# Norm before weights, and one more quad in seven products: a change to a decoder layer's order of work

## The chip, the core and the metric

The kernel runs on one NeuronCore of a Trainium2 chip. The core has five engines with queues of their own that meet only through semaphores: TensorE (PE, with its weight loads shown as PEld), VectorE (DVE), ScalarE (ACT), GpSimd (POOL) and SyncE (SP); in this kernel SP and POOL mainly issue DMAs. The metric is device time in microseconds of one execution. The profile is one execution, taken apart by a hardware profiler.

## The reference

One decoder layer on 256 tokens of width 2048, all in float32: a half-step SwiGLU feed-forward block, a mixer of two attention branches, and a second half-step feed-forward block, each followed by a residual sum and a layer norm.

```python
h = _layer_norm(ALPHA * h + 0.5 * _swiglu(h, ffn1_w_gate[l], ffn1_w_up[l], ffn1_w_down[l]), ln1_g[l], ln1_b[l])
mix = _mixer(h, ...)          # w_in, low-rank attention, differential attention, gates, w_out
h = _layer_norm(ALPHA * h + mix, ln2_g[l], ln2_b[l])
h = _layer_norm(ALPHA * h + 0.5 * _swiglu(h, ffn2_w_gate[l], ffn2_w_up[l], ffn2_w_down[l]), ln3_g[l], ln3_b[l])

def _swiglu(x, w_gate, w_up, w_down):
    return (jax.nn.silu(x @ w_gate) * (x @ w_up)) @ w_down
```

The hidden width of a feed-forward block (FFN) is 5632. Nearly all of the work is in products of the 256 tokens with large weight matrices, each of which is read once.

## The kernel before

**Precision and one product.** Every operand of a large product is split into a rounded part and a remainder, both in a faster 32-bit format: `split` (L151) lets ScalarE cast (L152, "CAST" in the profile) and VectorE subtract (L153). A product of two 128-blocks is then three matmuls, high by high, high by low, low by high: `triple`, L205, L206, L207. The split weights lie in `wring`, a ring of pairs of buffers; activations are called x, h, h1, y, xs in the profile (numbers are left out, so `h` there is a hidden quad of an FFN as well as the normed rows h1 and h2).

**Units.** The work is cut into units, one block of weights of 128x1024 each (two k-tiles of 128 by 512 columns). A unit has three steps: its load (on SP's queue), its preparation (the split, preceded by an add where blocks are combined) and its products. `unit`, `advance` and `look` (L170 to L195) let loads run three units and preparations four units ahead of the products. The two halves of the tokens are "blocks" b = 0 and b = 1 of 128 tokens. In `project` (L209) a unit's products for block 0 come at once, and those for block 1 are put into `behind` and follow up to LAG = 5 units later, so that block 0 of a layer's result is done well before block 1 and its norm can run beside the rest; `catch_up(n)` issues all but n of those left over. `later(n, fn)` runs fn after n more units have gone through. What is written in this order gets its final place on each engine from a planner, which simulates the engines and lets an instruction of lower rank go first if it would be ready sooner; `tc.issue_after(i)` forces that what is traced within stands behind instruction i on i's engine.

**Seven instead of eight.** Parts of the products use a scheme of Strassen's kind: a 2x2 product of blocks in seven block products instead of eight, with sums of the weights (VectorE, L405 in `Hybrid`, L595 in `Sliced`) and of the activations (`Seven`, `Extra`, `QuadForms`). `Hybrid` does the gate and up products and parts of the mixer. `Sliced` does an FFN's down product: 11 quads of the hidden width (a quad is 4 k-tiles of 128) in two passes p = 0 and p = 1 over half of the output columns each. In each pass quads 0 to 2 are in seven products ("s" in the string `mix`, 6 matmuls each) and the other eight in plain units ("p", 12 matmuls each); `order` gives the order of the seven products of a quad. A product's weight blocks "11", "12" and "22" lie in one buffer each (`self.R`), which products read and add to in place, and which is loaded again for the next quad once the last of them has read it. The rows of the hidden quads go through DRAM to be transposed and are fetched by `get_h` on POOL's queue; `split_h` splits them, `QuadForms.steps` makes the seven forms. In the last eight units of the second pass the blocks are apart as in `project`. `SLOTS` = 41 buffers are shared by all of the larger tiles.

**The norms.** `LayerNorm` holds the residual rows z, adds the results to them (`fold` L737, `evac` L749 and L751), counts (`bn_stats`, L754, L760) and, when a block's last part has come, runs `apply` (L764): mean and variance, `rstd` (L657: a square root on ScalarE, some small steps on VectorE), the normed rows (L784), then for each of the four quads of columns `rows_to_quad` (L644): four transposes on TensorE into a PSUM bank (L647; three banks), four scalings by gain and shift on ScalarE (L652), and the split into the next stage's x. `finish` (L788) makes the rows for the next residual sum (L790, L791). The norm's rows of gains and shifts are loaded on POOL's queue (L729) at the turns `at[1]`.

At the first FFN's end and after `w_out` the units of the next projection are written straight after the last ones, so the leftovers of block 1 alternate with the next projection's units, and block 1's norm is written five units later. `behind_x=3` holds back, in the second FFN's first projection alone, the splits of units 3 and later behind the split of the normed quad 0 of block 0 (`x.made[0, 0]`). In the mixer's groups over `Hybrid` with `small` set, the last results stand behind the last split (`behind_split`, L333).

## Time and profile before

| | us |
|---|---|
| median of three runs (1981.73 to 1983.7) | 1982.71 |
| the profiled execution's own time | 1981.89 |
| its span in the profile | 1979.8 |
| first norm: first transposes (L647) | 689.2 |
| second norm: second block's transposes (L647) | 1296.1 |
| second FFN's last unit's products end | 1969.1 |

The page gives for each engine its busy time, its share of the span and its number of instructions. A busy TensorE says that a matmul was under way, not that it ran at its peak; ends of matmuls are modelled, so lost time is better counted from the distance of their starts. Windows give the same numbers for a stretch of time, the waits say which instruction ended another engine's idle time, and the rows of the timeline merge neighbouring instructions of one kind (xN), with the idle time before them in brackets.

### The profile page before, as it was taken

To read this page: it belongs to the slowest core of one execution; us is meant where nothing else is said; L and a number is where in the kernel's file an instruction comes from. 1 tells how busy PE (TensorE), PEld (TensorE's weight loads), DVE (VectorE), ACT (ScalarE), POOL (GpSimd) and SP (SyncE) were. 2 spreads that over 40 slices of the span, in tenths; PEclk is the share of its full clock that TensorE was granted. 3 is DMA by queue.
4 is the path that set the end of the run, shared out by engine and by line. 5 is a ranking of instruction groups with operands and counts; after the bars stand their busy time and mean duration, and the time that the engine had idled before them with its cause. 6 is when DMAs were issued, how large, how long until landed. Compare 5 with 4: busy or idle time off the path is not lost.

```text
span 1979.8 us, 25620 instructions
## 1 busy us (share of the span) xinstructions
PE 1960.8 (99%) x8796; PEld 1621.2 (82%) x8796; DVE 1756.0 (89%) x2135; ACT 1261.4 (64%) x1637; POOL 294.3 (15%) x515
## 2 busy tenths in 40 slices
PE   9999999999999999999999999999999999999997
PEld 7888888888888798888788888878888888888886
DVE  7999999999998889998877676699999999989886
ACT  6666666766655566666667765566676666666552
POOL 0221112112100011002223120012112121121000
PEclk9999999999999999999999999999999999999999
DMA  8978888778777666677667667579888877787763
GB/s 303 292 234 272 273 257 252 226 221 316 252 231 260 216 214 242 220 250 250 219 209 249 232 216 273 183 245 289 240 290 268 243 241 238 214 323 256 245 214 125
DMA packets 144594, 484.63 MB, mean 245 GB/s; under 512 B 20640, under 2 KB 20688, under 8 KB 144464
## 3 DMA queue, kind: packets, MB, share of 16 engines
q1 hardware_dynamic: 112752, 389.60, 57.2%
q0 software_dynamic: 31712, 93.41, 17.7%
q8 instruction: 69, 1.13, 0.2%
q14 instruction: 61, 0.50, 0.1%
HBM read 454.08 MB, written 28.84 MB: 244 GB/s over the span
## 4 chain that ended last, share of the span: by engine, by line
PE 48%; DVE 3%; issue 1%; DMA 1%; ACT 1%; POOL 0%; DVEq 0%; POOLq 0%; ACTq 0%
PE mm L206 15%; PE mm L207 15%; PE mm L205 15%; DVE wring L153 2%; DVE sraw L405 1%; DMA turn<-blocks 1%; PE tr L205 0%; PE tr L207 0%; PE tr L206 0%; POOL turn L684 0%; ACT wring L152 0%; DMA turned<-turn 0%; DVE blocks L682 0%; PE tr L1229 0%; PE tr L1231 0%
## 5 line engine op out<-in xcount | busy, mean ns | idle before, releaser
L152 ACT CAST wring<-raw 128x1024 fp32r<-128x1024 f32 (+2 forms) x475 | 490.6, 1038 | 340.7 <-PE mm L207 249.4
L153 DVE TENSOR_TENSOR wring<-raw,wring 128x1024 fp32r<-128x1024 f32 (+2 forms) x475 | 566.9, 1200 | 121.1 <-ACT wring L152 118.1
L152 ACT CAST wring<-sraw 128x1024 fp32r<-128x1024 f32 x436 | 452.0, 1051 | 191.9 <-DVE sraw L405 76.5
L153 DVE TENSOR_TENSOR wring<-sraw,wring 128x1024 fp32r<-128x1024 f32 x436 | 520.9, 1218 | 26.7 <-ACT wring L152 24.6
L207 PE MATMUL mm<-wring,h 128*128 128x512 f32 (+2 forms) x1260 | 484.7, 385 | 0.0
L206 PE MATMUL mm<-wring,h 128*128 128x512 f32 (+2 forms) x1260 | 484.3, 385 | 0.1
L205 PE MATMUL mm<-wring,h 128*128 128x512 f32 (+2 forms) x1260 | 483.8, 385 | 0.4 <-ACT h L152 0.4
L206 PE MATMUL mm<-wring,xs 128*128 128x512 f32 x776 | 303.1, 391 | 1.8 <-DVE wring L153 1.2
L205 PE MATMUL mm<-wring,xs 128*128 128x512 f32 x776 | 302.3, 390 | 0.0
L207 PE MATMUL mm<-wring,xs 128*128 128x512 f32 x776 | 302.0, 389 | 0.0
L206 PEld LDWEIGHTS mm<-wring,h 128*128 128x128 f32 x1260 | 236.7, 188 | 47.7 <-DVE wring L153 1.4
L205 PEld LDWEIGHTS mm<-wring,h 128*128 128x128 f32 x1260 | 236.7, 188 | 47.4 <-ACT h L152 0.9
L207 PEld LDWEIGHTS mm<-wring,h 128*128 128x128 f32 x1260 | 236.7, 188 | 47.2 <-DVE h L153 0.7
L405 DVE TENSOR_TENSOR sraw<-sraw,sraw 128x1024 f32<-128x1024 f32 x168 | 199.3, 1217 | 3.5 <-DMA sraw<-in_wdv_dram 2.4
L206 PEld LDWEIGHTS mm<-wring,xs 128*128 128x128 f32 x776 | 145.7, 188 | 35.7 <-DVE wring L153 5.6
L205 PEld LDWEIGHTS mm<-wring,xs 128*128 128x128 f32 x776 | 145.7, 188 | 30.3
L207 PEld LDWEIGHTS mm<-wring,xs 128*128 128x128 f32 x776 | 145.7, 188 | 29.8
L206 PE MATMUL mm<-wring,x 128*128 128x512 f32 x348 | 135.9, 390 | 0.7 <-DVE wring L153 0.7
L205 PE MATMUL mm<-wring,x 128*128 128x512 f32 x348 | 135.1, 390 | 0.7 <-ACT wring L152 0.5
L207 PE MATMUL mm<-wring,x 128*128 128x512 f32 x348 | 135.3, 389 | 0.0
L684 POOL DMA_DIRECT2D hT<-blocks x176 | 96.8, 562 | 186.4 <-DVE blocks L682 186.4
L407 POOL DMA_DIRECT2D sraw<-in_gu_dram x40 | 35.5, 887 | 511.7 <-DVE sraw L405 406.2
(301 smaller groups left out, 2210.4 us busy)
## 6 DMA issues: line engine op xcount, KB each, us to landing
raw<-in_gu_dram SPq DMA_DIRECT2D x167, 512.0 KB, 5.1
sraw<-in_gu_dram SPq DMA_DIRECT2D x160, 512.0 KB, 5.3
raw<-in_dn_dram SPq DMA_DIRECT2D x140, 512.0 KB, 4.8
sraw<-in_gu_dram POOLq DMA_DIRECT2D x40, 512.0 KB, 7.0
sraw<-in_dn_dram SPq DMA_DIRECT2D x36, 512.0 KB, 6.2
hraw<-hT POOLq DMA_DIRECT2D x68, 256.0 KB, 5.7
raw<-in_w_out_dram SPq DMA_DIRECT2D x32, 512.0 KB, 4.3
eraw<-in_gu_dram SPq DMA_DIRECT2D x48, 256.0 KB, 5.7
```

The lines of the kernel that those rows point to most:

```text
L152: cast[0] = S.copy(hi, src)
L153: return V.tensor_tensor(out=lo, in0=src, in1=hi.bitcast(F32), op=ALU.subtract)
L205: PE.matmul(o, xh, wh, start=first, stop=False, skip_group_check=again)
L206: PE.matmul(o, xh, wl, start=False, stop=False, skip_group_check=again)
L207: PE.matmul(o, xl, wh, start=False, stop=last, skip_group_check=again)
L405: V.tensor_tensor(out=t, in0=t, in1=R[add[1]][s], op=ALU.add)
L407: nc.gpsimd.dma_start(R["12"][s], source("22", s), accum_op=ALU.add)
L684: nc.gpsimd.dma_start(to.rearrange("(g r) (i f) -> i r g f", g=4, i=4)[i], t[32 * i:32 * (i + 1), :].rearrange("r (g f) -> r g f", g=4))
```

## The change

Five things, all in one diff. (1) `catch_up(0)` at the end of an FFN and after `w_out`: all leftovers of block 1, and with them block 1's norm, are written before the next projection's units. A projection that follows a norm gets it as `norm`: its splits of units 3 to 6 stand behind block 0's first normed quad (on ScalarE behind block 0's square root, or its first cast), those of unit 7 and of the second FFN's next projection behind block 1's normed rows and square root. This now holds for the mixer's first projection too. (2) Quads 1 and 3 of the normed rows are scaled by two VectorE operations instead of four on ScalarE, quad 3's behind the split of quad 0. (3) In the second down pass quad 3 is the fourth quad in seven products, its hidden rows are fetched and its forms made ten to two units ahead; the mix is denser in products. (4) In both passes product 7 comes after 2 and 4. (5) The last norm rows are loaded at turns 102 to 108 instead of 94 to 103, and the square root's table at 38 instead of 35. Besides, only the gate groups of the mixer keep their last results behind a split.

```diff
-    def project(w, x, k_tiles, width, done, k0=0, hook=None, between=None, behind_x=None):
+    def project(w, x, k_tiles, width, done, k0=0, hook=None, between=None, norm=None, free=(3, 7)):
...
-                with tc.issue_after(x.made[0, 0].ins) if behind_x is not None and j >= behind_x else nullcontext():
+                waits = ()
+                if norm is not None and j >= free[0]:
+                    if j >= free[1]:
+                        waits = norm.applied[1], norm.root[1]
+                    else:
+                        waits = norm.x.made[0, 0], norm.root[0] if j == free[0] else norm.x.cast[0, 0]
+                with ExitStack() as stack:
+                    for i in waits:
+                        stack.enter_context(tc.issue_after(i.ins))
...
-                        with behind_split(1) if small else nullcontext():
+                        with behind_split(1) if gates else nullcontext():
...
-            for i in range(4):
-                k = 4 * q + i
-                S.activation(full[:, i * P:(i + 1) * P], t[:, i * P:(i + 1) * P], AF.Identity,
-                             bias=shift[:, k:k + 1], scale=gain[:, k:k + 1])
+            if q % 2 == 1:
+                v, o = (u.rearrange("p (i t) -> p i t", i=4) for u in (full, t))
+                g, b0 = (u[:, 4 * q:4 * q + 4].unsqueeze(2).to_broadcast([P, 4, P]) for u in (gain, shift))
+                with tc.issue_after(x.made[q - 3, b].ins) if q > 2 else nullcontext():
+                    V.tensor_tensor(out=v, in0=o, in1=g, op=ALU.mult)
+                V.tensor_tensor(out=v, in0=v, in1=b0, op=ALU.add)
+            else:
+                for i in range(4):
...
-                between=between, behind_x=3 if n == 2 else None)
-        project(wgu[1], x, KD, 512, lambda b, bank: gu_done(1, b, bank), hook=second)
+                between=between, norm=norm)
+        project(wgu[1], x, KD, 512, lambda b, bank: gu_done(1, b, bank), hook=second, norm=norm, free=(0, 0))
...
-        ln = LayerNorm(0.5, residual, g, bt, each, nxt, cols, ((24, 26, 48, 50), (94, 97, 100, 103)), 35)
+        ln = LayerNorm(0.5, residual, g, bt, each, nxt, cols, ((24, 26, 48, 50), (102, 104, 106, 108)), 38)
...
-        order = (1, 5, 6, 7, 2, 4, 3)
+        order = (1, 5, 6, 2, 4, 7, 3)
+        late = (3,)
...
-                rest = deque(quad_units((9, 10, 3, 4)) + [(m, 2 * q + i) for m in range(2) for q in (5, 6, 7, 8) for i in range(2)])
-                mix = "p" + "spspspspspspsppp" * 2 + "spspspspspss"
-            products = deque((q, f, None) for q in range(3) for f in order)
+                rest = deque(quad_units([q for q in (9, 10, 3, 4) if q not in late])
+                             + [(m, 2 * q + i) for m in range(2) for q in (5, 6, 7, 8) for i in range(2)])
+                mix = "p" + "sspspsspspsp" * 3 + "sspspsspsps"
+            products = deque((q, f, None) for q in (range(3) if p == 0 else (0, 1, 2) + late) for f in order)
...
             else:
+                for i, q in enumerate(late):
+                    call(units.index((i, order[-1], None)) + 10, lambda i=i: forms.pop(i))
+                    first_use = units.index((q, 1, None))
+                    call(first_use - 10, lambda q=q: get_h(q))
+                    forms[q] = QuadForms(spare)
+                    for i, fn in enumerate(forms[q].steps(lambda q=q: got[q])):
+                        call(first_use + (-6, -5, -4, -3, -2)[i], fn)
+                    call(first_use - 1, lambda q=q: got.pop(q))
                 call(len(units) - 8, widen)
...
         look(0, 0)
+        catch_up(0)
+        return ln
...
-        project(a["wc0"], x, KD, 512, cq_done)
+        project(a["wc0"], x, KD, 512, cq_done, norm=norm)
...
-                     False, f == 2)
+                     False, f == 2, True)
...
                 hook=at_unit(0, widen) if c == 3 else None)
+    catch_up(0)
```

28 lines of the change are left out of this document (19 added, 9 removed).

## The prediction

> **What bounds the kernel now.** I read the page first, for the engine shares:
>
> ```profile
> span 1979.8 us, 25620 instructions
> PE 1960.8 (99%) x8796; PEld 1621.2 (82%) x8796; DVE 1756.0 (89%) x2135; ACT 1261.4 (64%) x1637; POOL 294.3 (15%) x515
> ...
> L152 ACT CAST wring<-sraw 128x1024 fp32r<-128x1024 f32 x436 | 452.0, 1051 | 191.9 <-DVE sraw L405 76.5
> ```
>
> TensorE is busy 99% of the span (the cast's 1051 ns are used below). So only two things can change the time: the number of matmuls, and the moments at which TensorE stands still. Second, windows over the stages (columns: us, then busy time and instructions of PE, PEld, DVE, ACT, POOL, then clock, DMA share, GB/s):
>
> ```profile
> 800.00:900.00 100.00, 100.00 (x443) 82.81 (x442) 90.85 (x83) 62.87 (x67) 5.80 (x11) 1.00 0.73 248
> 100.00:200.00 100.00, 99.88 (x440) 82.27 (x439) 96.13 (x105) 69.20 (x86) 16.42 (x27) 1.00 0.83 255
> ...
> 688.30:702.05 13.75, 12.31 (x66) 9.38 (x65) 10.71 (x25) 9.84 (x27) 0.00 (x0) 1.00 0.15 39
> 1277.60:1299.10 21.50, 20.25 (x102) 15.66 (x100) 18.22 (x30) 14.88 (x33) 0.00 (x0) 1.00 0.52 172
> ...
> 688.70:692.30 3.60, 2.19 (x18) 1.74 (x17) 3.47 (x9) 2.45 (x7) 0.00 (x0) 1.00 0.49 134
> 1295.70:1299.20 3.50, 2.24 (x17) 1.69 (x17) 3.50 (x8) 2.43 (x7) 0.00 (x0) 1.00 0.36 131
> 1851.00:1946.00 95.00, 95.00 (x420) 78.67 (x420) 82.25 (x81) 55.14 (x58) 4.25 (x8) 1.00 0.70 232
> 1969.10:1979.80 10.70, 0.00 (x0) 0.00 (x0) 7.42 (x16) 0.20 (x1) 0.00 (x0) 0.74 0.36 134
> ```
>
> A matmul of 512 columns takes 100/443 = 0.226 us of TensorE at full clock (1.00). The second down pass of the second FFN (1851 to 1946, up to its last eight units) has no idle TensorE at all. The largest idle stretch, 10.7 us, is the last norm, which the change leaves as it is. The two inner norms show 3.60 - 2.19 = 1.41 and 3.50 - 2.24 = 1.26 us of idle. Third, what TensorE waited for in the whole run:
>
> ```profile
> PE tr L1156 <- ACT dkT L704: 1.0, 1, 1.0
> PE tr L647 <- DVE z L784: 0.9, 2, 0.5
> PE tr L647 <- ACT h1raw L652: 0.7, 1, 0.7
> PE tr L647 <- ACT h2raw L652: 0.7, 1, 0.7
> ```
>
> The waits at L647, the transposes of the normed rows, are those of the two inner norms. All in all there is little to win: about 20 us of idle, half of it at the end.
>
> **Part 1: the fourth quad in seven products.** In each second pass quad 3 goes from four plain units of 12 matmuls to seven products of 6: 48 become 42. Two FFNs: 12 matmuls x 0.226 = **-2.7 us**. This is certain as long as VectorE keeps up, and that has to be costed, since each of the seven products needs a split of its own and four of them an add:
>
> ```profile
> L153 DVE TENSOR_TENSOR wring<-sraw,wring 128x1024 fp32r<-128x1024 f32 x17 | 20.6, 1219 | 1.7 <-ACT wring L152 1.3
> L595 DVE TENSOR_TENSOR sraw<-sraw,sraw 128x1024 f32<-128x1024 f32 x8 | 9.8, 1222 | 0.2
> ...
> L506 DVE TENSOR_TENSOR f<-hraw,f 128x256 f32<-128x256 f32 x12 | 5.0, 418 | 0.1
> ...
> 1282.40 2.35 DVE L153 TENSOR_TENSOR wring<-raw,wring 128x1024 fp32r<-128x1024 f32 x2
> ```
>
> The last row gives the true price: two subtractions of 1.22 us end after 2.35 us, so one in a full queue costs 1.14, and every instruction about 0.08 less than its duration. Added per pass: three more splits and four more adds, 7 x 1.14 = 8.0; the forms of quad 3 (four differences and three splits of 128x256 at 0.42 - 0.08 = 0.34, two splits of twice that size at 0.60), 3.6. Together 11.6 us. VectorE's occupancy in the window is 82.25 - 81 x 0.08 = 75.8; it becomes 87.4 in 95.0 - 1.3 = 93.7 us, or 93%. Is that bearable? In the window 100 to 200, amid the gate and up products, it is 96.13 - 105 x 0.08 = 87.7% and TensorE loses 0.1 us. So a little beyond what the trace shows. There is also a reserve:
>
> ```profile
> ACT wring L152 <- PE mm L207: 29.5, 25, 3.0
> DVE wring L153 <- ACT wring L152: 11.6, 13, 1.5
> ```
>
> These waits (1850 to 1950) say that casts stand still until TensorE frees a pair of the ring: the splits are as far ahead as the ring lets them be. Four units prepared, of 92.5/48 = 1.93 us each in the new mix (28 products of 1.36 and 20 plain units of 2.71 us make 92.5), are 7.7 us of reserve. I take **+0.5 us** for both passes. The bounds: 0, and 5.2 us per pass, if VectorE's idle time can't be filled (rival B).
>
> [...]
>
> **The products' new order** (7 after 2 and 4) shortens the way from the last use of block "12" (product 7) to its next load (product 5 of the following quad) to five units, 7, p, 3, p, 1: 3 x 1.36 + 2 x 2.71 = 9.5 us of TensorE. The load waits for product 7's split, lands, and is added, cast and subtracted:
>
> ```profile
> sraw<-in_dn_dram SPq DMA_DIRECT2D x36, 512.0 KB, 6.2
> ```
>
> 6.2 + 1.2 + 1.05 + 1.2 = 9.7 us, so each of three seams takes 0.2 us out of the reserve of 7.7. On SP's queue the loads issued after it wait as well; they are for units behind it. In the first pass nine units lie between. Cost: nothing; without the reserve 0.6 us a pass.
>
> **Part 2: the inner norms.** VectorE at the first one:
>
> ```profile
> 681.45 0.68 DVE L751 SCALAR_TENSOR_TENSOR z<-mm,z 128x512 f32<-128x512 f32 x1
> 684.39 1.23 DVE L153 TENSOR_TENSOR wring<-raw,wring 128x1024 fp32r<-128x1024 f32 x1
> 686.15 1.23 DVE L153 TENSOR_TENSOR wring<-raw,wring 128x1024 fp32r<-128x1024 f32 x1 [0.21 <-issue]
> 687.37 1.22 DVE L153 TENSOR_TENSOR wring<-raw,wring 128x1024 fp32r<-128x1024 f32 x1
> 688.50 1.91 DVE L784 TENSOR_SCALAR z<-z,mv,f 128x512 f32<-128x512 f32 x4
> 690.33 0.68 DVE L751 SCALAR_TENSOR_TENSOR z<-mm,z 128x512 f32<-128x512 f32 x1
> 697.23 0.16 DVE L667 RECIPROCAL y<-sd 128x1 f32<-128x1 f32 x1 [0.39 <-ACT sd L661]
> 698.40 1.92 DVE L784 TENSOR_SCALAR z<-z,mv,f 128x512 f32<-128x512 f32 x4
> ```
>
> Splits of the mixer's new weights sit between block 0's last accumulation (681.45) and its normed rows (688.50): 7.05 us. At the second norm, where the old code already holds units 3 and later back, the same chain takes 1274.24 to 1277.43, 3.19 us:
>
> ```profile
> 1274.24 0.69 DVE L749 TENSOR_TENSOR z<-mm,z 128x512 f32<-128x512 f32 x1 [1.77 <-PE mm L207]
> 1277.43 1.92 DVE L784 TENSOR_SCALAR z<-z,mv,f 128x512 f32<-128x512 f32 x4
> 1291.65 0.69 DVE L749 TENSOR_TENSOR z<-mm,z 128x512 f32<-128x512 f32 x1 [0.29 <-PE mm L207]
> 1295.47 1.91 DVE L784 TENSOR_SCALAR z<-z,mv,f 128x512 f32<-128x512 f32 x4
> 1296.08 1.57 PE L647 MATMUL tr<-ident,z 128*128 128x128 f32 x12 [0.38 <-DVE z L784]
> 1298.33 0.66 PE L647 MATMUL tr<-ident,z 128*128 128x128 f32 x4 [0.69 <-ACT h2raw L652]
> ...
> 689.19 1.50 PE L647 MATMUL tr<-ident,z 128*128 128x128 f32 x12 [0.48 <-DVE z L784]
> 692.27 0.50 PE L205 MATMUL mm<-wring,h 128*128 128x512 f32 x1 [0.20 <-ACT h L152]
> ```
>
> With units 3 and up held, block 0's rows at the first norm can be ready at 681.45 + 3.19 + 0.5 (a fourth of 1.91) = 685.1 instead of 689.0, while TensorE still has second halves of down until 688.7 (689.19 - 0.48). The first new product follows the transposes by 692.27 - 689.19 = 3.1 us, so it could run at 688.2; the second halves and the transposes (1.9 us) fill TensorE until about 690.6. It starts then instead of at 692.27.
>
> At the second norm the trouble is block 1: its accumulation ended only at 1291.65, because TensorE had taken all 48 products of block 0 with the first new weights (8 units x 6) in among the leftover second halves, and had nothing left when the rows came at 1296. Run before them, the 30 leftovers (6.8 us) and block 0's transposes (1.9) end at about 1282.9, counted from 1274.24, and the chain (3.2 to 8.1 us, the far end from 690.33 to 698.40) runs beside 8 x 1.36 = 10.9 us of block-0 products. At the first norm block 1 gains from the moved scaling: its square root waited for ScalarE, which was busy with sixteen scalings of block 0.
>
> That scaling, quads 1 and 3 on VectorE, is an operation the trace doesn't have. Two tensor-tensors of 128x512, one from PSUM: nearest is z<-mm,z with 0.69, so 2 x 0.60 to 2 x 0.69 = 1.2 to 1.4 us a quad; ScalarE's four take 1.54 (row below). In latency that is even or a little better; in load some 3 us per block leave ScalarE and 2.4 to 2.8 come to VectorE, beside the new splits. Quad 3's scaling, queued behind quad 0's split, holds up only work that is needed two quads later.
>
> ```profile
> 1299.01 1.54 ACT L652 ACTIVATE h2raw<-tr,cols 128x128 f32<-128x128 f32 x4
> ```
>
> What it can bring: the idle rows, 1.41 + 1.26 = 2.7 us, at the least if all goes; the window 688.30 to 702.05 holds 66 starts, 32 of them transposes at 1.50/12 = 0.125 us, 34 x 0.226 + 32 x 0.125 = 11.7 of 13.75 us, so 2.1 us are lost; the window 1277.60 to 1299.10 in the same way 21.5 - 70 x 0.226 - 32 x 0.125 = 1.7; 3.8 us at the most. The other bound is a loss: the split of unit 3 now stands behind block 0's first quad, and behind it queue the splits of units 4 to 6, then unit 7 and the next weights after block 1. If block 1's chain (8.1 us) came first, TensorE would run out after three units (4.1 us) and lose 4.0 instead of 2.1 and 1.7: +4.2 in all. I take **-3.0 us** for both, between the two gains, since some short waits at the transposes will stay (four tiles, three PSUM banks).
>
> **Edits with one answer, nothing.** Norm rows later: their turns go from 94 to 103 of 106 units to 102 to 108 of 109, so they come two to five units, at most 14 us, nearer to the end; the last was issued at 1929.75 (row below), 39 us before TensorE's last matmul. POOL's queue then passes quad 3's reload first, and nothing else waits there. The square root's table moves by three units with the pass. The mixer's last results no longer stand behind a split in the three query, key and value groups: it may free the wait of 1.0 us at L1156, or put two 0.60 us results ahead of a split in each group, 3.6 us at most; with both signs open I take 0.
>
> ```profile
> 1929.75 0.53 POOL L729 DMA_DIRECT2D gb<-in_ln_b_dram  x1 [16.97 <-DVE wring L153]
> ```
>
> **Sum.** -2.7 + 0.5 - 3.0 = -5.2 us on the profiled execution's own 1981.9 (span 1979.8 and 2.1 around it), so 1976.7. That execution is 0.8 below the median of the runs, 1982.7; against the median the forecast is **1977.5 us**.
>
> **Rivals.** *A, the norms' waits only move:* the transposes stay in TensorE's order where they stand, the fourth again waits for ScalarE to free a bank, and block 1's chain is stretched by 2.4 us more of scaling on VectorE. For it: both 0.7 us waits are of this kind and no edit adds a bank. Against it: the cover of 10.9 us. Time: 1982.7 - 2.7 + 0.5 = 1980.5; with the starved unit 3 of part 2 it is 1980.5 + 4.2 = 1984.7. *B, VectorE sets the pace of the second passes:* its idle 12.7 us of the window are waits for casts (11.6 us in 13 waits) that stay when the work grows. Then it needs 95.0 + 11.6 = 106.6 us against 93.7 + 7.7, TensorE is late by 5.2 us in each pass, and the time is 1982.7 - 2.7 - 3.0 + 10.4 = 1987.4. TensorE is late once more than 7.5 of the 12.7 us stay unfilled, and the whole is slower than before once 10.4 do. Against it: casts there wait for TensorE, 29.5 us, so the idle time is a full ring. *C, everything goes:* all 3.8 us at the norms and the 1.0 us at L1156, no new wait: 1982.7 - 2.7 - 4.8 = 1975.2. *D, the change doesn't do what it says:* the planner orders instructions by its own costs, so held-back splits may stand no differently; that is A's time.
>
> **Chances.** Forecast 0.50; A and D 0.27; B 0.14; C 0.09. What a measurement tells from no change, 0.2%, is 4.0 us: faster is below 1978.7, slower above 1986.7. Faster: C, and most of the forecast (1975.5 to 1979.5) with 0.46: 0.55. Same: the rest of the forecast, A, and the milder half of B: 0.34. Slower: 0.11. The range takes in C, A's worse end and some way to B: 1974 to 1985.5; the likeliest case's own is 1975.5 to 1979.5.
>
> **What would show it.** 8784 matmuls instead of 8796; a second pass whose TensorE stays full while VectorE's busy time in it rises by about 12 us; the first transposes of the first norm some 4 us after block 0's last accumulation, not 7.7 (681.45 to 689.19); at the second norm block 1's accumulation before most of the new products. I am wrong if TensorE waits for the splits inside the second passes (B), or if the waits at L647 keep their idle 2.7 us (A).

## The result, and the profile after

The change made the kernel slower: 1991.2 us against 1981.8 us, the medians of six runs each, ratio 1.0050 with a 95% interval of 1.0038 to 1.0063. The forecast was 1977.5. The profiled execution took 1994.0 us with a span of 1992.1; before it was 1981.9 and 1979.8. The changed kernel's profiled execution is the longest of its six, 2.8 us above their median, so up to that much of what its trace shows as lost is not in the median.

The page of the changed kernel, its span and its engines (busy time, share, instructions):

```profile
span 1992.1 us, 25570 instructions
...
PE 1963.0 (99%) x8784; PEld 1619.7 (81%) x8784; DVE 1782.9 (89%) x2179; ACT 1257.2 (63%) x1617; POOL 294.4 (15%) x515
```

The 8784 matmuls are there, twelve fewer than before. What TensorE waited for in the whole run (line, releaser, us, times, longest):

```profile
PE mm L208 <- DVE wring L155: 9.6, 9, 2.5
PE mm L207 <- ACT wring L154: 3.6, 3, 2.9
PE tr L208 <- DVE wring L155: 2.0, 3, 0.8
...
PE tr L657 <- DVE z L804: 0.3, 2, 0.2
```

The waits at the transposes of the normed rows (now L657) are down to 0.3 us; those were the target of part 2, and both waits for ScalarE there are gone. But the waits for splits have grown to 15.2 us: L155 is VectorE's subtraction and L154 ScalarE's cast. In the kernel before they were 2.4 us, 0.5 of them for a cast and the rest for subtractions (L206 and L153 there):

```profile
PE mm L206 <- DVE wring L153: 1.9, 5, 0.7
```

Windows put the losses in four places. The changed kernel (us, then busy time and instructions of PE, PEld, DVE, ACT, POOL, then clock, DMA share, GB/s):

```profile
600.00:668.00 68.00, 65.44 (x283) 52.63 (x283) 63.42 (x71) 43.61 (x50) 3.18 (x6) 1.00 0.68 235
...
710.00:740.00 30.00, 28.02 (x187) 26.05 (x187) 28.12 (x53) 16.96 (x29) 8.78 (x16) 1.00 0.77 243
740.00:770.00 30.00, 27.93 (x138) 23.33 (x137) 28.11 (x50) 18.67 (x28) 4.34 (x8) 1.00 0.69 240
770.00:800.00 30.00, 28.90 (x128) 23.60 (x127) 27.81 (x27) 17.83 (x19) 2.20 (x4) 1.00 0.76 272
...
1340.00:1360.00 20.00, 16.35 (x62) 12.16 (x61) 14.81 (x14) 11.52 (x14) 4.98 (x9) 0.91 0.88 266
...
1853.00:1956.00 103.00, 102.22 (x451) 84.33 (x450) 90.16 (x92) 58.75 (x65) 3.18 (x6) 1.00 0.59 202
1956.00:1984.00 28.00, 22.97 (x101) 18.35 (x99) 21.98 (x36) 4.98 (x7) 0.00 (x0) 1.00 0.33 113
```

The same stretches of the kernel before, as far as they were not shown:

```profile
600.00:668.00 68.00, 68.00 (x302) 56.31 (x301) 59.38 (x63) 40.66 (x42) 2.37 (x5) 1.00 0.72 240
...
710.00:740.00 30.00, 30.00 (x208) 28.85 (x207) 25.30 (x47) 18.11 (x29) 6.28 (x12) 1.00 0.84 285
740.00:770.00 30.00, 29.91 (x138) 24.32 (x137) 29.99 (x51) 20.40 (x30) 4.34 (x8) 1.00 0.67 227
770.00:800.00 30.00, 29.67 (x131) 24.19 (x130) 28.53 (x28) 17.78 (x19) 2.20 (x4) 1.00 0.67 243
```

The first FFN's second down pass (600 to 668) idles for 2.6 us where it had none. The mixer's start (710 to 800) idles for 30 - 28.02 + 30 - 27.93 + 30 - 28.90 = 5.2 us against 0.4. The second FFN's first seven-product group (1340 to 1360) idles for 3.7 us, and the second FFN's second down pass for 0.8 us up to 1956 and some 2.5 behind it (of the 5.0 us in the last row the other 2.5 lie after TensorE's last matmul).

Idle time is not all of the loss. Counted in matmul starts, the window 600 to 668 is short of 302 - 283 = 19, or 4.3 us at 0.226 us each, and the window 1340 to 1360 of 90 - 62 = 28, or 6.3 us. In the second of these windows part of the reason is the granted clock, 0.91 instead of 1.00. TensorE stood still from 1346.97 to 1349.86 and for 0.8 us more behind the next matmul, and just after that its granted clock reads 0.50, with matmuls 0.43 us apart instead of 0.23:

```profile
1352.00:1354.00 2.00, 2.00 (x6) 1.51 (x6) 1.11 (x1) 2.00 (x3) 2.00 (x4) 0.50 0.46 114
```

How the loss after the second norm comes about can be followed over VectorE, GpSimd and ScalarE (start, duration, engine, line, operation; in brackets the idle time ahead and what ended it). VectorE, changed kernel:

```profile
1331.23 0.69 DVE L811 TENSOR_TENSOR z<-z,gb 128x512 f32<-128x512 f32 x1
...
1336.71 2.36 DVE L415 TENSOR_TENSOR sraw<-sraw,sraw 128x1024 f32<-128x1024 f32 x2
...
1349.84 1.23 DVE L155 TENSOR_TENSOR wring<-sraw,wring 128x1024 fp32r<-128x1024 f32 x1 [3.66 <-ACT wring L154]
```

GpSimd's queue and ScalarE, the same kernel:

```profile
1338.49 0.90 POOL L417 DMA_DIRECT2D sraw<-in_gu_dram  x1 [5.74 <-PE mm L208]
1339.70 0.86 POOL L417 DMA_DIRECT2D sraw<-in_gu_dram  x1 [0.32 <-issue]
...
1347.33 1.04 ACT L154 CAST wring<-sraw 128x1024 fp32r<-128x1024 f32 x1 [4.02 <-PE mm L209]
```

The norm's last multiplications and additions (L810, L811) run until 1331.9, one directly after another with the splits. So the group's block additions (L415) come at 1336.71, the two accumulating loads behind them are issued at 1338.49 and 1339.70, the cast of their block starts at 1347.33, VectorE has meanwhile stood idle for 3.66 us, and TensorE for 2.9. In the kernel before those loads were issued at 1329.92 and 1331.13. (The trace names a matmul as the cast's releaser. The two loads landed 8.5 and 11.1 us after their issue, though, which puts the first landing at 1347.0, and the cast started at 1347.33.)

In the second down pass the changed kernel shows this on VectorE (L605 is the addition of two blocks of weights):

```profile
1909.18 1.23 DVE L605 TENSOR_TENSOR sraw<-sraw,sraw 128x1024 f32<-128x1024 f32 x1 [2.19 <-DMA sraw<-in_dn_dram]
...
1929.30 1.23 DVE L155 TENSOR_TENSOR wring<-sraw,wring 128x1024 fp32r<-128x1024 f32 x1 [3.67 <-ACT wring L154]
1931.27 1.23 DVE L605 TENSOR_TENSOR sraw<-sraw,sraw 128x1024 f32<-128x1024 f32 x1 [0.75 <-DMA sraw<-in_dn_dram]
1933.77 1.22 DVE L605 TENSOR_TENSOR sraw<-sraw,sraw 128x1024 f32<-128x1024 f32 x1 [1.27 <-DMA sraw<-in_dn_dram]
```

and on ScalarE the cast at 1928.22 had waited 3.95 us for such a load. A block of weights is reloaded only after the last reader of the quad before, and while the instruction that needs it waited, its engine ran nothing else, as these idle times show.

### The profile page after: what moved, and what is told of

Its sections match the earlier page's. It is cut to its first block, busy times and chain, and to the rows that moved or that the text cites. A ratio compares the mean times of both kernels' runs of the same rounds, so it can differ in the third digit from the quotient of the medians.

```text
span 1992.1 us, 25570 instructions
## 1 busy us (share of the span) xinstructions
PE 1963.0 (99%) x8784; PEld 1619.7 (81%) x8784; DVE 1782.9 (89%) x2179; ACT 1257.2 (63%) x1617; POOL 294.4 (15%) x515
## 4 chain that ended last, share of the span: by engine, by line
PE 52%; DVE 11%; DMA 4%; issue 3%; ACT 2%; POOL 0%; DVEq 0%; ACTq 0%
PE mm L208 16%; PE mm L209 16%; PE mm L207 16%; DVE wring L155 5%; DMA sraw<-in_dn_dram 2%; ACT wring L154 1%; DVE sraw L415 1%; DVE sraw L605 1%; PE tr L657 0%; DMA raw<-in_dn_dram 0%; DMA sraw<-in_gu_dram 0%; DVE blocks L701 0%; PE tr L208 0%; DVE z L810 0%; PE tr L209 0%
## 5 line engine op out<-in xcount | busy, mean ns | idle before, releaser
L154 ACT CAST wring<-raw 128x1024 fp32r<-128x1024 f32 (+2 forms) x469 | 484.6, 1037 | 299.7 <-PE mm L209 200.1
L155 DVE TENSOR_TENSOR wring<-raw,wring 128x1024 fp32r<-128x1024 f32 (+2 forms) x469 | 560.1, 1200 | 88.9 <-ACT wring L154 85.6
L154 ACT CAST wring<-sraw 128x1024 fp32r<-128x1024 f32 x448 | 464.1, 1051 | 236.3 <-DVE sraw L415 81.1
L155 DVE TENSOR_TENSOR wring<-sraw,wring 128x1024 fp32r<-128x1024 f32 x448 | 536.1, 1220 | 47.5 <-ACT wring L154 46.4
L208 PE MATMUL mm<-wring,h 128*128 128x512 f32 (+2 forms) x1228 | 472.7, 385 | 5.2 <-DVE wring L155 5.1
L209 PE MATMUL mm<-wring,h 128*128 128x512 f32 (+2 forms) x1228 | 472.6, 385 | 0.0
L207 PE MATMUL mm<-wring,h 128*128 128x512 f32 (+2 forms) x1228 | 470.6, 385 | 0.0
L208 PE MATMUL mm<-wring,xs 128*128 128x512 f32 x792 | 310.2, 392 | 4.7 <-DVE wring L155 3.9
L207 PE MATMUL mm<-wring,xs 128*128 128x512 f32 x792 | 309.0, 390 | 3.4 <-ACT wring L154 3.4
L209 PE MATMUL mm<-wring,xs 128*128 128x512 f32 x792 | 308.8, 390 | 0.0
L208 PEld LDWEIGHTS mm<-wring,h 128*128 128x128 f32 x1228 | 230.6, 188 | 53.4 <-DVE wring L155 7.7
L207 PEld LDWEIGHTS mm<-wring,h 128*128 128x128 f32 x1228 | 230.6, 188 | 45.7 <-ACT h L154 0.7
L209 PEld LDWEIGHTS mm<-wring,h 128*128 128x128 f32 x1228 | 230.6, 188 | 45.2 <-DVE h L155 0.2
L415 DVE TENSOR_TENSOR sraw<-sraw,sraw 128x1024 f32<-128x1024 f32 x168 | 199.3, 1219 | 2.8 <-DMA sraw<-in_wdv_dram 1.7
L208 PEld LDWEIGHTS mm<-wring,xs 128*128 128x128 f32 x792 | 149.0, 188 | 40.7 <-DVE wring L155 9.8
L207 PEld LDWEIGHTS mm<-wring,xs 128*128 128x128 f32 x792 | 148.9, 188 | 35.4 <-ACT wring L154 4.4
L209 PEld LDWEIGHTS mm<-wring,xs 128*128 128x128 f32 x792 | 149.0, 188 | 30.3
L208 PE MATMUL mm<-wring,x 128*128 128x512 f32 x348 | 135.9, 390 | 0.5 <-DVE wring L155 0.5
L207 PE MATMUL mm<-wring,x 128*128 128x512 f32 x348 | 135.0, 390 | 0.2 <-ACT wring L154 0.2
```

Of the source, the lines that this page charges most:

```text
L154: cast[0] = S.copy(hi, src)
L155: return V.tensor_tensor(out=lo, in0=src, in1=hi.bitcast(F32), op=ALU.subtract)
L207: PE.matmul(o, xh, wh, start=first, stop=False, skip_group_check=again)
L208: PE.matmul(o, xh, wl, start=False, stop=False, skip_group_check=again)
L209: PE.matmul(o, xl, wh, start=False, stop=last, skip_group_check=again)
L415: V.tensor_tensor(out=t, in0=t, in1=R[add[1]][s], op=ALU.add)
```

## The experiments

The first four runs share their runs of the kernel before (median 1981.9 us), the next four theirs (1981.6), the following three (1981.6) and the last three (1981.6) likewise.

**Scaling back on ScalarE.** Edit:

```diff
-            if q % 2 == 1:
+            if False:
                 v, o = (u.rearrange("p (i t) -> p i t", i=4) for u in (full, t))
```

> The changed kernel with the scaling of quads 1 and 3 at both inner norms back on ScalarE (four activations a quad, as before); waits, order and second passes as changed. Theory 1 (VectorE has no free time after the norms: 16 scaling operations of 0.60 us, 4.8 us a norm, push the norms' finish, the splits and the reloads behind them late): the idle TensorE time after the norms (5.5 us in the mixer at 726 to 800, 6 us at 1340 to 1400) goes, the time is 1991 - 11 = about 1980 us, and the stalls inside the second passes stay. Rival 2 (it is the held-back splits of units 3 and up that arrive late, wherever the scaling is done): TensorE's idle time at those places stays and the time is over 1988 us.

Measured: 1980.3 us, ratio to before 0.9992 (0.9983 to 1.0001). TensorE's waits in the whole run of this kernel:

```profile
PE mm L208 <- DVE wring L155: 3.2, 4, 1.4
...
PE mm L207 <- ACT wring L154: 0.8, 1, 0.8
```

and its windows:

```profile
710.00:740.00 30.00, 30.00 (x207) 28.77 (x206) 26.77 (x50) 18.62 (x31) 7.04 (x13) 1.00 0.85 289
740.00:770.00 30.00, 29.28 (x135) 23.74 (x134) 29.05 (x50) 19.05 (x29) 4.34 (x8) 1.00 0.67 232
770.00:800.00 30.00, 28.57 (x127) 23.28 (x126) 28.20 (x28) 17.45 (x19) 2.20 (x4) 1.00 0.68 246
...
1340.00:1360.00 20.00, 20.00 (x90) 16.55 (x89) 18.74 (x19) 13.59 (x17) 4.00 (x8) 1.00 1.00 366
```

Theory 1 holds: 11 us come back with this one edit, all of the 3.7 us at 1340 with the clock of 0.50 behind them, and 3 of the 5.2 in the mixer. Rival 2 would have kept them. One thing was not expected: the stall at the end of the second FFN's down pass was gone too, in a pass whose code is the same. Each trace is one execution, and the changed kernel's was 2.8 us above its median, so whether the scaling has to do with that stall stays open.

**The old second passes.** Edit (the norm rows and the root's table go back to their old turns too):

```diff
-        ln = LayerNorm(0.5, residual, g, bt, each, nxt, cols, ((24, 26, 48, 50), (102, 104, 106, 108)), 38)
+        ln = LayerNorm(0.5, residual, g, bt, each, nxt, cols, ((24, 26, 48, 50), (94, 97, 100, 103)), 35)
...
-        order = (1, 5, 6, 2, 4, 7, 3)
-        late = (3,)
+        order = (1, 5, 6, 7, 2, 4, 3)
+        late = ()
...
-                mix = "p" + "sspspsspspsp" * 3 + "sspspsspsps"
+                mix = "p" + "spspspspspspsppp" * 2 + "spspspspspss"
```

> The changed kernel with both second down passes as before: three quads in seven products, the old mix and product order, norm rows and root table at their old turns; the norms as changed. Theory (the second passes lost 7 us of TensorE time and saved 2.7 us of matmuls): 1991 - 4.3 = about 1987 us, 8796 matmuls, no idle TensorE over 0.3 us in the passes. Rival (the whole loss comes from the norms, and stalls in a pass would only have come later): no change, 1991 to 1994 us.

Measured: 1987.9 us, 1.0029 (1.0018 to 1.0039). The pass costs 3.3 us inside the changed kernel, and the loss after the norms does not need it: `PE mm L207 <- ACT wring L154: 3.2, 2, 3.0` stands in this kernel's waits too.

**Both undone.** Edit: the two above together.

> Both undone: scaling on ScalarE and second passes as before; what remains of the change is the waits that hold new weights back at the inner norms, the second halves caught up ahead of the mixer and the second FFN, and the unheld results in the gate and up groups with the mixer's held. Theory 1: the gains stay without the losses: norm waits 5.4 to about 0.6 us, and the mixer's 2 us at 950 to 962: 1982 - 5 = 1976 to 1978 us. Rival 2 (held splits are late): over 1984 us, with idle TensorE time at 720 to 800 and 1340 to 1400 us.

Measured: 1978.5 us, 0.9981 (0.9972 to 0.9989), faster than before. The waits at the norms' transposes are 0.3 us, and TensorE has no wait over 0.5 us at 1300 to 1400. At 740 to 800 it still loses some:

```profile
740.00:770.00 30.00, 28.92 (x130) 23.18 (x129) 29.65 (x51) 20.33 (x29) 4.35 (x8) 1.00 0.65 219
770.00:800.00 30.00, 28.37 (x126) 23.10 (x125) 27.62 (x27) 16.81 (x18) 2.20 (x4) 1.00 0.67 242
```

With these three runs the whole difference between the two kernels is taken apart: holds and unheld results 1978.5 - 1981.9 = -3.3 us; scaling, with the holds, 1987.9 - 1978.5 = +9.4; the passes, on top of both, 1991.2 - 1987.9 = +3.3. The sum is +9.4 us, which is what was measured. The parts depend on the order in which they are taken: in the kernel with the fourth quad the scaling is worth 1991.2 - 1980.3 = 10.9 us, and without the scaling the passes cost 1980.3 - 1978.5 = 1.8.

**No reloads in the second passes.** Edit:

```diff
                 load_block, src, other, key = plan[p]
+                again = tail > 0 and q > 0 and load_block in R
+                if again:
+                    self.reads[load_block] = uses[load_block]
+                    load_block = None
```

> The changed kernel; left out are the reloads of blocks 11, 12 and 22 for quads 1 to 3 in the second down passes (the products of these quads use the first quad's blocks as they stand; every add, cast and split remains). Theory 3 (the stalls in the second passes come from reload seams: a single buffer is reloaded only after the former quad's last reader, and the add that waits for it holds VectorE's queue): the 3.3 and 3.6 us of idle TensorE time in the passes fall below 0.5 us each, time 1991 - 6 = about 1985 us. Rival B (VectorE's work alone, 93% of the pass, sets the pace): the stalls stay, 1990 to 1993 us.

Measured: 1985.7 us, 1.0019 (1.0010 to 1.0028). The first FFN's pass:

```profile
600.00:668.00 68.00, 68.00 (x301) 56.33 (x301) 65.97 (x77) 45.83 (x53) 3.19 (x6) 1.00 0.60 200
```

TensorE is full although VectorE does as much as in the changed kernel (busy 1783.0 us in the whole run against 1782.9) and works for 65.97 of the 68 us here. In this pass VectorE's load alone therefore did not make the stalls; without the reloads it keeps up. (The edit takes away the waits and, with them, nine loads a pass on SP's queue; this run does not tell the two apart.) The losses after the norms stayed, as they should: this kernel still scales on VectorE.

**The mixer's weights not held back.** Edit, on the kernel with both undone:

```diff
-    yq = mixer(h1, ln1)
+    yq = mixer(h1, None)
```

> The kernel of the run before with both undone (1978.5 us), and the mixer's new weights not held back at the first norm; the second norm's waits stay. Theory: the hold at the first norm saves its 2.8 us of waits and gives back 1.3 us at 700 to 750 and 1.8 us at 750 to 800 as later splits, so it is worth nothing: the time stays within 1 us of 1978.5, with the idle time again at the first norm's transposes (some 2.5 us at 680 to 700) and about 1.5 us at 700 to 800 us. Rival (the hold is a true gain and the loss at 750 to 800 comes from the second halves caught up ahead of the mixer): the time rises by 2.5 us or more, and 750 to 800 still loses 3 us.

Measured: 1978.75 us, 0.9982 (0.9973 to 0.9991), the same as with the hold. TensorE's waits from 675 to 800 us:

```profile
PE mm L208 <- DVE wring L155: 1.0, 1, 1.0
PE tr L657 <- ACT h1raw L669: 0.7, 1, 0.7
PE tr L657 <- DVE z L804: 0.5, 1, 0.5
```

With the hold this stretch has `PE mm L208 <- DVE wring L155: 2.7, 3, 1.6` and 0.2 us at the transposes. The hold at the first norm moves a stall of its own size to a place 60 to 100 us later. At this norm the waits only moved, as rival A has it, though not by A's mechanism: the transposes themselves no longer wait.

**Two second buffers.** Edit, on the kernel with the scaling back:

```diff
+            if tail > 0:
+                self.other = {**self.R, **{n: act_tile([P, 1024], F32, "sraw") for n in ('12', '22')}}
+            sets = [self.R, self.other or self.R]
...
+                R = sets[q % 2]
```

> The changed kernel with the scaling back on ScalarE (1980.3 us) and, in the second down passes, a second buffer for blocks 12 and 22, used by quads 1 and 3, so that their reloads need not wait for the last reader of the quad before; all work as in the changed kernel. Theory 3 (reload seams): the 3.4 us lost in the first FFN's second pass go, 1980.3 - 3.4 = about 1977 us, and the reserve of prepared splits in the second FFN's pass stays above 3 us instead of falling to 1.5. Rival B (VectorE's work): no change, 1979 to 1981 us. Third case (the extra buffers take slots from the loads of the down inputs): over 1982 us.

Measured: 1979.3 us, 0.9991 (0.9982 to 1.0000), 1 us better than without, not 3.4. A miss: the stalls of the first FFN's pass stayed (TensorE is busy for 65.7 of the 68 us from 600 on). VectorE is busy for 66.7 us there, so it has next to no room left. On ScalarE the cast of block 11, the one that still had a single buffer, waits for its reload (in the second FFN's pass for up to 3.14 us, but there TensorE lost nothing):

```profile
614.29 1.05 ACT L154 CAST wring<-sraw 128x1024 fp32r<-128x1024 f32 x1 [1.96 <-DMA sraw<-in_dn_dram]
```

**The unheld results alone.** Edit on the kernel before: only the mixer's three gate groups keep their results behind a split.

```diff
-                        with behind_split(1) if small else nullcontext():
+                        with behind_split(1) if gates else nullcontext():
```

> The kernel before with one edit: the last results of the mixer's query, key and value groups no longer stand behind a split. Theory: this alone takes away the stalls at 950 to 962 us (2.0 us idle before), 1982 - 2 = 1980 us. Rival (the held norms shifted the mixer's work, and that removed them): no change, 1982 us, with the stalls still there.

Measured: 1980.35 us, 0.9995 (0.9986 to 1.0004): by the time it can't be told from no change. The trace shows the mechanism: from 945 to 965 us TensorE is busy for 20.00 us in this kernel and for 18.26 in the kernel before, and the waits at L1156 and L206 there are gone.

**The scaling alone.** Edit: the kernel before with the changed kernel's scaling of quads 1 and 3 on VectorE.

> The kernel before with one edit: quads 1 and 3 of the two inner norms are scaled on VectorE. Theory 1 (VectorE is full after the norms whatever the waits are, so 4.8 us more a norm come out as idle TensorE time): 1982 + 8 to 11 = 1990 to 1993 us, idle TensorE time at 720 to 800 and 1340 to 1400 us. Rival (it costs only together with the held-back splits): 1981 to 1984 us.

Measured: 1987.6 us, 1.0029 (1.0017 to 1.0040). It is 6 us on its own and 9.4 with the holds, so theory 1 has the right sign, but the amount is below its range, and the place is another one: here the second norm itself is late. TensorE's only wait over 0.1 us from 1270 to 1400 us:

```profile
PE tr L647 <- DVE z L791: 3.2, 1, 3.2
```

The splits that the scaling has pushed back now stand in block 1's chain: from its last accumulation (1293.02) to its rows (1299.62) it takes 6.6 us, with three splits in between, where before it took 3.8 with one. What makes up the rest of the 6 us was not shown. With the holds that wait is covered, and the work left over appears as the stall at 1346.

**Three second buffers.** Edit: as with two, with `('11', '12', '22')`.

> As the run with a second buffer for blocks 12 and 22, now with one for block 11 too. In that run ScalarE's cast of the next quad's first product still waited 3.14 us for block 11's reload at 1890 us, and 2.9 us of idle TensorE time stayed in the first FFN's second pass. Theory 3 in its wider form (all three blocks' reloads are seams, and VectorE at 93% cannot catch up between them): no product waits for a reload over 1 us, the 2.9 us go, the reserve in the second FFN's pass stays above 4 us, time about 1976.5 us. Rival B (VectorE's work): still 1979 to 1981 us, stalls as before.

Measured: 1981.5 us, 0.9996 (0.9987 to 1.0004). A miss in the time: the first FFN's pass is full from 600 us on, but at its start, 576 to 580 us, TensorE now loses 3.5, by the distance of its starts. From 560 to 668 us this kernel's waits are:

```profile
PE tr L207 <- ACT wring L154: 1.8, 1, 1.8
PE tr L208 <- DVE wring L155: 1.3, 1, 1.3
```

**Less work on VectorE.** Edit, on the kernel with the scaling back; it leaves out the subtractions of the plain units with both halves together:

```diff
-                    split(*pair, st["raw"])
+                    if tail > 0 and not apart:
+                        S.copy(pair[0], st["raw"])
+                        pair = (pair[0], pair[0])
+                    else:
+                        split(*pair, st["raw"])
```

> The changed kernel with the scaling back on ScalarE (1980.3 us); left out are the subtractions of the plain units in the second down passes up to their last eight units (TensorE's second matmul of a triple reads the rounded weights again): some 17 us less on VectorE in the part with products, TensorE's work and all reloads unchanged. If seams alone make the stalls, the 3.4 us in the first FFN's second pass stay: 1980 us. If VectorE's load of 93% is needed for them too (a seam takes 2 to 5 us out of the reserve, and only a VectorE with spare time builds it up again), they fall under 1 us: 1977 us, and the reserve in the second FFN's pass is back above 4 us ahead of each seam.

Measured: 1990.8 us, 1.0044 (1.0032 to 1.0056). The time can't be used: at the first norm new waits of 7.2 and 5.3 us appeared; where they come from stays open. The pass itself answers the question:

```profile
600.00:668.00 68.00, 68.00 (x302) 56.31 (x301) 50.55 (x52) 43.79 (x46) 2.12 (x4) 1.00 0.73 251
```

VectorE has 13 us less to do, TensorE is full, and the waits for reloads are still there: 1.72 us at 616 and 0.91 at 638 on VectorE. So here a reload's wait did no harm, with VectorE busy for only 50.55 of the 68 us. The reverse is shown less well: without reloads the load did no harm, but with three second buffers TensorE lost 3.5 us at 576 although no reload was waited for. There VectorE had set-up work to do, in it a wait of 1.22 us for a load of the set-up's own. The measure of the reserve that the expectation speaks of needs a split in every unit and was not read here.

**The second passes alone.** Edit: the kernel before with the fourth quad, mix, product order and later norm rows.

> The kernel before with the second down passes alone as changed (fourth quad, mix, product order, norm rows and root table later); norms and mixer as before. Theory: 12 matmuls less, 2.7 us, against 3.4 us of stalls in the first FFN's pass and 0 to 3.6 us in the second's: 1982.5 to 1986 us. My forecast's step for this part: 1982 - 2.2 = about 1979.5 us.

Measured: 1984.7 us, 1.0012 (1.0004 to 1.0021), inside the theory's range and 5 us above my forecast's step. In its profile the first FFN's pass idles for 2.4 us, the second FFN's for none, and the first norm is later than before:

```profile
600.00:668.00 68.00, 65.64 (x284) 52.82 (x284) 63.62 (x71) 43.74 (x50) 3.18 (x6) 1.00 0.70 236
```

```profile
PE tr L647 <- DVE z L784: 2.8, 2, 2.3
```

0.9 us at the norms' rows became 2.8.

**The mixer's set-up earlier.** Edit, on the kernel with the scaling back:

```diff
-            later(70, setup)
+            later(30, setup)
```

> The changed kernel with the scaling back on ScalarE (1980.3 us), and the set-up of the mixer's tables (masks, biases, angles, sines) moved from turn 70 to turn 30 of the first FFN's down part, into the first pass, where VectorE has more free time. If the first FFN's pass stalls because this work comes on top of the fourth quad's there (VectorE 38.3 of 40 us busy at 600 to 640), the 3.4 us fall under 1 us and the time is about 1977.5 us. If the reload seams alone do it, the 3.4 us stay: 1980 us.

Measured: 1978.4 us, 0.9983 (0.9973 to 0.9992), 1.9 us better than without it and faster than both kernels of this study. Its pass is read from the last run below, which has the same one.

**Three second buffers and the set-up earlier.** Both edits.

> The same with second buffers for blocks 11, 12 and 22 in the second passes. In the run with these buffers and the set-up at its old turn, 3.5 us of idle TensorE time appeared at 576 us, where VectorE worked on set-up and the first norm's sums while the add of product 5 was due. If set-up work caused that, it goes too: no idle TensorE time in either pass, 1976.5 to 1977.5 us. If the extra buffers caused it (three of 41 slots, so a later start of other loads), it stays: 1980 to 1981.5 us.

Measured: 1978.5 us, 0.9986 (0.9977 to 0.9995), as without the buffers. Of the 3.5 us at the start of the first FFN's pass about 1 is left; the set-up was most of it.

**Set-up earlier, mixer's weights not held back.**

> The run with the set-up moved alone, and the mixer's new weights not held back at the first norm. If the hold is worth nothing, as in the pair of runs without the fourth quad (1978.5 and 1978.75 us), the time is within 1 us of the run with the set-up moved; if the hold matters more with the fourth quad, whose pass hands over a smaller reserve, it is 2 us or more above.

Measured: 1980.2 us, 0.9993 (0.9984 to 1.0002), 1.8 us above the run with the hold, between the two cases. Its first FFN's pass:

```profile
600.00:668.00 68.00, 68.00 (x302) 56.31 (x301) 61.51 (x62) 41.03 (x44) 2.11 (x4) 1.00 0.65 230
```

No idle TensorE, with VectorE busy for 61.5 us instead of 63.7 (scaling back, set-up late). So the set-up's load, on top of the fourth quad's, is why the first FFN's pass stalled. It does so in every kernel where both met, but for the one without reloads and the one with less work on VectorE. In the second FFN's pass, where there is no set-up, this run lost `PE mm L208 <- DVE wring L155: 2.1, 1, 2.1`, while the other kernels with the fourth quad, the changed one apart, lost nothing there. What decides that from run to run stays open; in the changed kernel the loads of these blocks landed after 4.4 to 11.8 us, median 6.1.

## Why the prediction was wrong

**Bounds of the kernel.** Right: TensorE at 99%, so only matmuls and moments of standing still count. What I read too lightly is the other half of that page, VectorE at 89%. I looked for places where VectorE's work is late, not for places where it has no room.

**Part 1, the matmuls.** 12 x 0.226 = -2.7 us: right, 8784 matmuls. **VectorE's load:** the three splits, four adds and the forms are there, but the 93% was too low. A window's busy time counts two instructions that overlap only once: the durations of the 81 instructions from 1851 to 1946 add up to 86.6 us, and the window says 82.25. I took 0.08 us per instruction off the 82.25, where the overlap was already out. From 86.6 it leaves 80.1, and 11.6 more make 91.7 of 93.7 us, 98%; the comparison from 100 to 200 is at 96%, not 87.7. The run with three second buffers and the set-up earlier, in which nothing in the second FFN's pass waits for a reload, is near that, 90.94 of 94 us:

```profile
1852.00:1946.00 94.00, 94.00 (x416) 77.82 (x416) 90.94 (x94) 61.02 (x67) 5.31 (x10) 1.00 0.65 224
```

TensorE is full in it, so it can live with that load, but hardly anything is left to make up for a wait. **"+0.5 us for both passes":** wrong, the second step that failed. The passes alone cost +3.1 us (1984.7 against 1981.6), where the step said -2.2: with 2.7 us of matmuls saved, 5.8 were lost in place of 0.5. Besides the load, three things were missing. First, the window 1851 to 1946 was taken for both FFNs, but the first FFN's pass also carries the mixer's set-up; moving that set-up took the stalls away. Second, the seam: I priced one block, "12", at "0.2 us out of the reserve per seam" with the median landing. Block 22 has five units too and block 11 six, a landing took up to 11.8 us, and the waiting addition or cast holds up all splits queued behind it: 2.19, 3.67, 0.75 and 1.27 us of idle VectorE in the changed kernel. Third, I took the reserve of 7.7 us as a stock that is there at each seam; at 98%, with 2.0 us free in 93.7 (an estimate, from the 91.7 above), VectorE needs much longer to refill it than the seams lie apart. And a smaller reserve at the end of the pass is handed on: with the pass alone the first norm's waits for rows grew from 0.9 to 2.8 us, which no step of mine had (that it is the reserve is argued, not shown).

**The price of 1.14 us.** The row was right: in the changed kernel two subtractions of 1.22 us again take 2.36 us together (from 1332.97). The use I made of it was wrong, as the load above shows.

**Part 2, the holds.** The mechanism is right at both norms. The first transposes come 3.5 us after block 0's last accumulation (forecast 4, before 7.7):

```profile
682.96 0.69 DVE L771 SCALAR_TENSOR_TENSOR z<-mm,z 128x512 f32<-128x512 f32 x1 [0.86 <-PE mm L209]
685.78 1.92 DVE L804 TENSOR_SCALAR z<-z,mv,f 128x512 f32<-128x512 f32 x4
```

```profile
686.48 1.50 PE L657 MATMUL tr<-ident,z 128*128 128x128 f32 x12 [0.16 <-DVE z L804]
```

My worry, TensorE starved by a late unit 3, did not come true. Without the scaling, holds and unheld results together gave -3.3 us, near the -3.0 taken for the holds and the 0 for the results. That is luck in part: the results' run alone had 1.25 us, within the noise, and the holds' share is smaller. At the first norm they are worth 0.2 us (1978.75 against 1978.5) without the fourth quad, because the stall turns up again at 740 to 800, and 1.8 us with it. At the second norm the order is as forecast. TensorE starts its last product with w_out's weights at 1289.58 and the first with the new ones at 1289.81, and block 1's accumulation on VectorE follows block 0's by 12.3 us:

```profile
1279.46 0.69 DVE L769 TENSOR_TENSOR z<-mm,z 128x512 f32<-128x512 f32 x1 [1.77 <-PE mm L209]
...
1291.78 0.68 DVE L769 TENSOR_TENSOR z<-mm,z 128x512 f32<-128x512 f32 x1
```

Before, it followed by 17.4 us (1274.24, 1291.65). It stands no earlier in absolute time because the changed kernel is 5 us behind by then.

**The failed step: scaling on VectorE at nothing.** The forecast said that 2.4 to 2.8 us a block come to VectorE and that this "holds up only work that is needed two quads later". The size was right: eight operations a norm of 0.68 us in steps of 0.60 make 4.8 us. The cover was not there. The changed kernel's VectorE from 1286 on:

```profile
1286.44 0.68 DVE L664 TENSOR_TENSOR h2raw<-tr,cols 128x512 f32<-128x512 f32 x1
...
1287.64 0.68 DVE L665 TENSOR_TENSOR h2raw<-h2raw,cols 128x512 f32<-128x512 f32 x1
...
1288.84 1.22 DVE L155 TENSOR_TENSOR wring<-raw,wring 128x1024 fp32r<-128x1024 f32 x1
```

This goes on, instruction after instruction, to 1340. The kernel before was already at 52.09 of 54 us there:

```profile
1286.00:1340.00 54.00, 52.73 (x239) 43.14 (x238) 52.09 (x75) 34.84 (x55) 6.13 (x10) 1.00 0.73 249
```

With 1.9 us of room, 4.8 us more had to come out somewhere: not in the quads that are scaled, but 50 us later, in the norm's finish, the additions for the seven products and the loads behind them. It cost 9.4 us for both norms with the holds and 6.0 without, where the sum had nothing. Part of that goes with the granted clock: from 1340 to 1360 it reads 0.91 in the changed kernel, and 1.00 in the kernel before, with the scaling back and with both undone. ScalarE, from which the work was taken, was busy for 34.84 of the 54 us and had room. That the scaling costs this much is shown by taking it out and by putting it in alone; that it costs it as load is read from the traces. No run keeps the load and drops the forced place of quad 3's scaling behind quad 0's split.

Against the same runs of the kernel before, -5.2 us were forecast and +9.4 measured. Of the 14.6 us between them the scaling makes 9.4 and the passes 5.5 (+3.3 instead of -2.2); the holds, with the unheld results, came out 0.3 better than the sum had them.

**Edits at nothing.** The unheld results took the wait at L1156 away, as hoped for; the time shows 1.25 us, within what can't be told from none. The later norm rows and the table showed no effect of their own; they were not tried apart.

**Rivals.** None had the right mechanism in full. B named the right stage, and its sign for the first FFN; its condition, that casts' waits can't be filled, came about through the reloads and the set-up on top of the load. My own sign for B, TensorE waiting for splits inside the second passes, did show. At the first norm the waits moved, as A has it, but not by A's mechanism. The cost of the scaling stood in A as "2.4 us more" in one chain, and never as a load on a full engine.

## What to carry to other kernels

When work moves to another engine, look up the receiving engine's busy share in the stretch where the work will run and in the 50 us after it, not only the latency of the piece that moves: here an engine at 96% paid for the added microseconds later, at whatever was queued last. Before correcting a window's busy time for overlaps, add up the durations in it and see whether they are already out. A reserve of prepared work is a rate and not only a stock: ask how long the engine needs to refill it, and how far apart the waits lie that empty it. And where one window stands for two passes of the same code, check that the second one has nothing else running beside it.

## What the hardware showed that I had not expected

The same 512 KB load into a block of weights landed after 4.4 to 11.8 us in one run of the changed kernel (median 6.1), so a distance of 9.5 us that covers the median is not a cover. A tensor-tensor that reads PSUM and a broadcast column operand took 0.68 us for 128x512 (L664), and so did one with plain operands from SBUF (L811). One wait of TensorE cost more than its length: in the changed kernel the window 1340 to 1360 has 3.7 us of idle time, and 6.3 us are lost by its starts. Behind waits of 2.89 us (up to 1349.86) and 0.76 us (up to 1351.12) the granted clock read 0.50 from 1352 to 1354, with matmuls 0.43 us apart instead of 0.23, and 1.00 again from 1356. Behind the wait of 2.49 us up to 1966.42, in the same kernel, it stayed at 1.00. What decides it was not shown. Three kernels with different mixes of the edits (holds and unheld results; fourth quad with earlier set-up; the same with three more buffers) ended within 0.2 us of each other, 1978.4 to 1978.5 us, all faster than before with intervals that end below 1.
